# Hybrid decoder step on one core: the loads at the start on one queue in order of use, and the FFN's entry on VectorE

## The chip, the core and the metric

The kernel runs on 1 core of one Trainium2 chip. The metric is the time of one execution in device microseconds (us); the time of a kernel is the median of its runs. A profiled execution gives the trace, and the profile is read from it. The engines of the core are TensorE (PE: matmuls, and PEld: its weight loads), VectorE (DVE), ScalarE (ACT), GpSimd (POOL) and SyncE (SP), which here only issues DMAs.

## The reference

One layer of a decoder, for 256 prompt tokens and 8 x 8 sample tokens (320 in all), with D = 2048, a mixed width of 4096 and d_ff = 5632. All weights and inputs are float32.

```python
h    = rms_norm(x, norm_mix_pre)
proj = h @ w_in                                  # gMLP u | gMLP v | z | xBC | dt
gate_out, chunk_v = chunk_spatial_gate(gelu(u), gelu(v), ...)   # layer norm of v, 128-token mixing
ssm_out, states   = ssd_mixer(z, conv(xBC), dt, ...)            # Mamba-2 SSD, exact
mix = concat([gate_out, ssm_out]) @ w_out
x   = x + rms_norm(mix, norm_mix_post)
up, new_conv = causal_depthwise_conv(rms_norm(x, norm_ffn_pre) @ ffn_w_up, ...)
f   = (gelu_tanh(g) * u) @ ffn_w_down            # g, u = halves of up
x   = x + rms_norm(f, norm_ffn_post)
```

The outputs are x for prompt and sample tokens, the SSM states, the last rows of both convolutions and of v.

## The kernel before

**Tiling.** Activations stand transposed: 128 rows of a feature block by 320 tokens, so D is 16 blocks ("k-tiles", KD). A product needs float32 accuracy, so activations and weights are split into a high and a low part. A weight piece of up to 512 KB (a *slab*, `slab`, L108 to L119) is loaded by SyncE into `wraw` (L115, 3 buffers), cast by ScalarE to `whi` (L117, 3 buffers), and VectorE subtracts to get `wlo` (L119, 3 buffers). For each 128 x 128 block of it, `accumulate` runs three matmuls over 320 columns: whi by x hi (L128), whi by x lo (L129), wlo by x hi (L130). `project` runs one output group of 4 blocks (512 columns), slab by slab along k; a slab is 2 k-tiles by 4 blocks or 4 k-tiles by 2 blocks, that is 24 matmuls. PSUM has 4 banks for groups (`mm`) and 4 for the rest (`ms`).

**Order of the stages.** In-projection (gMLP v, then u and the SSD inputs), gMLP and SSD mixing, `w_out` in 8 chunks (`chunk_out`), the second root-mean-square root, the FFN's entry, 11 FFN groups of 512 + 512 columns, the last norm and the output. Each norm's factor is per token, so it commutes with the projection: the products run on the unscaled x, and the factor (`r1`, `r3`) is multiplied in when a PSUM bank is evacuated.

**What sets the order.** A scheduler places instructions by priority; `first()` and `tc.high_priority` raise it, and `tc.issue_after(i)` puts an instruction behind `i` on the same engine (it does nothing between two engines). Background tasks (`bg`, `tick`) are generators of which one step is emitted after each slab. Instructions of one engine, DMA issues among them, go out in order; a slab's DMA waits for its `wraw` buffer, which VectorE's `wlo` of three slabs before sets free.

**The start.** `ones` is filled and EARLY matmuls (L70, each two in the trace) keep TensorE busy until data is there. x (transposed, 2.63 MB) comes in six DMAs of 1, 1, 2, 4, 4, 4 k-tiles on ScalarE's queue (L523 to L529), the weight slabs on SyncE's. `x_ready` (L533) splits each k-tile of x: ScalarE `h_hi` (L537), VectorE `h_lo` (L538). The first `project` runs 4 slabs of one k-tile, 4 of two, and the last four k-tiles in two slabs, 192 matmuls. x by token (2.62 MB, six loads into `acc_mix`, `bT` and `cT`, needed for the first norm's squares) is loaded by GpSimd through the software queue (`load_by_token`, L548 to L552). A small copy of `h_hi` in k-tile 8 stands ahead of each load, so that they start after that split. `with_r1` squares them (L557), takes the root, spreads it over the partitions and evacuates the first group.

**Roots.** `rsqrt_of` works on VectorE alone. `rsqrt_by_root` (L237) uses ScalarE's square root, whose table has to be loaded first. `root_table(pd_last[-1])` asks for a tiny square root (`root_there`) behind a matmul of TensorE, so as to have the table there in time.

**The FFN's entry.** With `r2b`, the second root spread to all partitions, `x1_ready` (L975) makes x1 = acc * norm * r2b + x for each k-tile: VectorE scales (L980); the add of x (L981) is VectorE's for k-tiles 0 and 1 and GpSimd's for the other 14; then `split` makes ScalarE's `h_hi` (L346) and VectorE's `h_lo` (L347). `project(ffn_w_up, 0, ..., more=DFF)` runs six blocks (288 matmuls) while this goes on. ScalarE squares each k-tile of x1 (L281) for the third norm; the sums go to two totals, even k-tiles to `sq3` by GpSimd and odd ones to `sq3b` by VectorE (L282), behind the add of k-tile 11. `ffn_up(0)` goes on with the seventh block (`ps_one`) and the eighth (`ps_other`); in the seventh stand the token sums of both totals (L263, `tsum`), the third root, its spread to `r3`, and the evacuation (`evac`) of the first seven blocks.

In both stages GpSimd also has small work: pads of the convolution (L1017, L1018), and in the entry four updates of sample states (L1120).

Of the kernel before, what the change touches and what calls it, by code (L numbers as in the profile page):

```python
# [28 lines left out]
EARLY = 10  # L29
# [5 lines left out]
def hybrid_step(  # L35
# [201 lines left out]
    def rsqrt_by_root(rest, ps, scale, rows=P):  # L237

        v = tp.tile([P, 3], F32, tag="rs_v3", name="rs_v")[:rows]
        r = tp.tile([P, 3], F32, tag="rs_r3", name="rs_r", bufs=3)[:rows]  # L240
        t = tp.tile([P, 3], F32, tag="rs_t3", name="rs_t")[:rows]
        s = tp.tile([P, 3], F32, tag="rs_s3", name="rs_s")[:rows]
        dve.tensor_scalar(out=v, in0=rest, scalar1=scale, scalar2=EPS, op0=ALU.mult, op1=ALU.add)
        dve.scalar_tensor_tensor(out=v, in0=ps, scalar=scale, in1=v, op0=ALU.mult, op1=ALU.add)
        act.activation(s, v, AF.Sqrt)
# [30 lines left out]
    def add_square(total, x, begins, adder=pool, place=("sq", 2)):  # L276
        if begins:
            act.activation(total, x, AF.Square)
        else:
            sq = tp.tile([P, NT], F32, tag=place[0], name="sq", bufs=place[1])  # L280
            act.activation(sq, x, AF.Square)  # L281
            adder.tensor_tensor(out=total, in0=total, in1=sq, op=ALU.add)  # L282

    def squares_of(total):
# [3 lines left out]
        def step(nb):  # L288
            if nb < KD - 3:
                add_square(total, acc[:, nb, :], nb == 0)  # L290
                return
            with first():
                if nb < KD - 1:
                    held.append(misc("sq_ps")[:, :NT])
                else:
                    one.append(tp.tile([P, NT], F32, tag="sq", name="sq", bufs=2))
                act.activation((one or held)[-1], acc[:, nb, :], AF.Square)
                if nb > KD - 3:
                    dve.tensor_tensor(out=total, in0=total, in1=held.pop(0), op=ALU.add)
# [40 lines left out]
    def split(hi, lo, x, scale=None):  # L340
# [4 lines left out]
        else:  # L345
            act.activation(hi, x, AF.Copy, scale=scale)  # L346
            dve.scalar_tensor_tensor(out=lo, in0=x, scalar=scale, in1=hi.bitcast(F32), op0=ALU.mult, op1=ALU.subtract)  # L347

# [19 lines left out]
    with ExitStack() as mctx:  # L368
# [141 lines left out]
        with tc.tile_pool(name="gp", bufs=1) as gp:  # L510
# [11 lines left out]
            k = 0  # L522
            with tc.high_priority(offset=300000):  # L523
                for n in (1, 1, 2, 4, 4, 4):
                    cs = slice(KD + NT * k if k else 0, KD + NT * (k + n))
                    act.dma_start(flat[:, cs], xT[:, cs])
                    k += n
                    if k == 2:
                        act.activation(held, ones[:, 0:1], AF.Square)  # L529
# [3 lines left out]
            def x_ready(k0, nk):  # L533
                with tc.high_priority(offset=100000):
                    for kt in range(k0, k0 + nk):
# [11 lines left out]
            by_tok += [(t.rearrange("p k n -> p (k n)")[64:, :D // 2], slice(64, P), slice(NP, NT), 2, i) for i, t in enumerate((bT, cT))]  # L547
            def load_by_token():  # L548
# [27 lines left out]
            load_by_token()  # L576

            def with_r1():
                yield
# [114 lines left out]
        with tc.tile_pool(name="sd", bufs=1) as sd:  # L694
# [250 lines left out]
            root_table(pd_last[-1])  # L945
# [7 lines left out]
            with first():  # L953
# [6 lines left out]
                r = rsqrt_by_root(most, ps, 1.0 / D)  # L960
# [8 lines left out]
            xr, added = {}, []  # L969
# [5 lines left out]
            def x1_ready(k0, nk):  # L975
                for kt in range(k0, k0 + nk):
                    q, k = kt // 4, kt % 4
                    a = acc[:, kt, :]
                    with first() if kt < 2 else tc.high_priority(offset=100000):
                        dve.scalar_tensor_tensor(out=a, in0=a, scalar=col(prm_at["norm"][0] + kt), in1=r2b, op0=ALU.mult, op1=ALU.mult)  # L980
                        added.append((dve if kt < 2 else pool).tensor_tensor(out=a, in0=a, in1=xr[q][:, k, :], op=ALU.add).ins)  # L981
                        split(hT[0][:, kt, :], hT[1][:, kt, :], a, col(prm_at["norm"][1] + kt))
# [13 lines left out]
    with tc.tile_pool(name="fp", bufs=1) as fp:  # L996
# [5 lines left out]
        def ffn_up(g):  # L1002
# [41 lines left out]
            if g == 0:  # L1044

                ps = misc("ps_one")
                for i in range(2):
# [92 lines left out]
        for g in range(NG):  # L1140
# [5 lines left out]
            if g == NG - 1:  # L1146
                finish(grow)
                root_table(pd_last[-1])
# [19 lines left out]
        r = rsqrt_by_root(most, ps, 1.0 / D)  # L1168
# [108 lines left out]
```

## Time and profile before

| what | value |
|---|---|
| median of 3 runs | 1811.83 us (1809.76 to 1812.11) |
| profiled execution, its own time | 1812.42 us |
| its span (first to last instruction) | 1810.7 us |
| TensorE matmuls busy | 1784.3 us (99%) |
| VectorE, ScalarE, GpSimd busy | 1183.4, 798.7, 303.2 us |
| mean DMA rate | 169 GB/s |

How to read the profile: a group's row gives line, engine, operation, output and inputs, shapes and count, then the busy time and the mean ns of one, then the idle time of the engine before them and what ended it. A row of the chain of waits gives a start, a length and the work that the next step waited for; a row of the timeline gives start, length, engine, line and operation, and in brackets the idle time before it with its releaser. In the table by stretches each engine has its busy time and its number of instructions, then come TensorE's granted clock, the share of the DMA engines' time and the GB/s. Matmuls are pipelined, so a matmul is shown longer than its distance from the next.

### The profile page before, as it was taken

The numbers are of one execution on the slowest core, as the hardware profiler recorded it, in microseconds if no ns is written. First come the engines' busy times: TensorE is split into PE (matmuls) and PEld (weight loads), VectorE is DVE, ScalarE is ACT, GpSimd is POOL, SyncE is SP. The second block draws the span as 40 slices with busy tenths as digits, with TensorE's granted clock in tenths as the row PEclk, the third lists the DMA queues.
The fourth block names the chain that finished last, engine by engine and source line by source line (L and its number), as shares of the span: only waits on it lengthen the run. The fifth ranks groups of instructions, "written<-read, shape, count | busy, mean of one in ns | idle before, by whom it ended". The sixth has DMA issues, their size and how long they took to land.

```text
span 1810.7 us, 31220 instructions
## 1 busy us (share of the span) xinstructions
PE 1784.3 (99%) x12222; PEld 1750.2 (97%) x12222; DVE 1183.4 (65%) x2033; ACT 798.7 (44%) x1106; POOL 303.2 (17%) x624
## 2 busy tenths in 40 slices
PE   8999999999999999999999999999999999999998
PEld 7999999999999898998899999999999999999997
DVE  4449565556867778577776575757665565756575
ACT  6444454334535354445455444344434343433335
POOL 2102110000120111005622212121201020101004
PEclk9999999999999999999999999999999999999999
DMA  8545544445764644454556656565654444444442
GB/s 269 178 149 176 173 137 152 152 151 162 244 197 154 192 161 150 137 178 150 161 163 201 196 191 211 174 202 177 194 175 151 147 153 150 155 152 153 149 153 99
DMA packets 229779, 306.46 MB, mean 169 GB/s; under 512 B 17440, under 2 KB 152704, under 8 KB 229440
## 3 DMA queue, kind: packets, MB, share of 16 engines
q1 hardware_dynamic: 216384, 279.26, 48.5%
q10 hardware_dynamic: 11024, 18.10, 2.7%
q0 software_dynamic: 2224, 7.11, 1.4%
q8 instruction: 96, 1.57, 0.4%
q14 instruction: 51, 0.42, 0.1%
HBM read 286.85 MB, written 17.58 MB: 168 GB/s over the span
## 4 chain that ended last, share of the span: by engine, by line
PE 93%; DVE 2%; DMA 2%; ACT 1%; POOL 1%; issue 1%; ACTq 0%; DVEq 0%; POOLq 0%
PE ps L128 19%; PE ps L130 19%; PE ps L129 19%; PE pd L128 10%; PE pd L130 10%; PE pd L129 10%; DMA wraw<-in_w_in 1%; PE y_ps L851 1%; DVE wlo L119 1%; POOL acc_mix L981 1%; PE yo_ps L804 1%; ACT whi L117 0%; PE sg L658 0%; PE up_ps L1128 0%; PE xt_ps L357 0%
## 5 line engine op out<-in xcount | busy, mean ns | idle before, releaser
L119 DVE TENSOR_TENSOR wlo<-wraw,whi 128x1024 fp32r<-128x1024 f32 (+1 forms) x476 | 591.4, 1243 | 409.1 <-ACT whi L117 406.1
L117 ACT CAST whi<-wraw 128x1024 fp32r<-128x1024 f32 (+1 forms) x476 | 496.8, 1044 | 721.1 <-PE ps L129 443.4
L128 PE MATMUL ps<-h_hi,whi 128*128 128x320 f32 x2528 | 790.2, 313 | 11.0 <-ACT whi L117 7.6
L130 PE MATMUL ps<-h_hi,wlo 128*128 128x320 f32 x2528 | 786.5, 311 | 4.0 <-DVE wlo L119 4.0
L129 PE MATMUL ps<-h_lo,whi 128*128 128x320 f32 x2528 | 785.1, 311 | 0.0
L128 PEld LDWEIGHTS ps<-h_hi,whi 128*128 128x128 f32 x2528 | 477.8, 189 | 17.6 <-ACT whi L117 9.2
L130 PEld LDWEIGHTS ps<-h_hi,wlo 128*128 128x128 f32 x2528 | 477.8, 189 | 6.1 <-DVE wlo L119 5.9
L129 PEld LDWEIGHTS ps<-h_lo,whi 128*128 128x128 f32 x2528 | 477.8, 189 | 1.2 <-issue 0.5
L128 PE MATMUL pd<-fhi,whi 128*128 128x320 f32 x704 | 218.0, 310 | 0.0
L129 PE MATMUL pd<-flo,whi 128*128 128x320 f32 x704 | 217.9, 310 | 0.0
L130 PE MATMUL pd<-fhi,wlo 128*128 128x320 f32 x704 | 217.9, 309 | 0.0
L128 PE MATMUL pd<-ohi,whi 128*128 128x320 f32 x448 | 140.6, 314 | 0.0
L129 PE MATMUL pd<-olo,whi 128*128 128x320 f32 x448 | 139.0, 310 | 0.0
L130 PE MATMUL pd<-ohi,wlo 128*128 128x320 f32 x448 | 138.7, 310 | 0.0
L129 PEld LDWEIGHTS pd<-flo,whi 128*128 128x128 f32 x704 | 132.2, 188 | 0.7
L130 PEld LDWEIGHTS pd<-fhi,wlo 128*128 128x128 f32 x704 | 132.2, 188 | 0.0
L128 PEld LDWEIGHTS pd<-fhi,whi 128*128 128x128 f32 x704 | 132.2, 188 | 0.0
L211 DVE TENSOR_TENSOR acc_ffn<-acc_ffn,pd 128x320 f32<-128x320 f32 x160 | 77.1, 483 | 35.8 <-PE pd L130 34.8
L1032 POOL COPY ptf<-pad 128x2 f32<-128x2 f32 x88 | 23.0, 263 | 390.7 <-DVE pad L1020 390.0
L128 PEld LDWEIGHTS pd<-ohi,whi 128*128 128x128 f32 x448 | 84.1, 188 | 4.0 <-issue 2.5
L130 PEld LDWEIGHTS pd<-ohi,wlo 128*128 128x128 f32 x448 | 84.1, 188 | 0.6 <-issue 0.6
L129 PEld LDWEIGHTS pd<-olo,whi 128*128 128x128 f32 x448 | 84.2, 188 | 0.2 <-issue 0.2
(296 smaller groups left out, 1596.1 us busy)
## 6 DMA issues: line engine op xcount, KB each, us to landing
wraw<-in_ffn_w_up SPq DMA_DIRECT2D x176, 512.0 KB, 3.5
wraw<-in_w_in SPq DMA_DIRECT2D x144, 512.0 KB, 3.5
wraw<-in_ffn_w_down SPq DMA_DIRECT2D x88, 512.0 KB, 3.3
wraw<-in_w_out SPq DMA_DIRECT2D x64, 512.0 KB, 3.3
st<-in_state_ssm SPq DMA_DIRECT2D x64, 256.0 KB, 3.7
out_ssm_state_sample<-st ACTq DMA_DIRECT2D x32, 256.0 KB, 2.5
cs<-dacs_d SPq DMA_DIRECT2D x16, 320.0 KB, 3.5
xr<-in_xT SPq DMA_DIRECT2D x4, 640.0 KB, 4.6
```

The costliest lines, as they stand in the source:

```text
L117: act.copy(hi[:, :m], raw[:, :m])
L119: dve.tensor_tensor(out=lo[:, :m], in0=raw[:, :m], in1=hi[:, :m].bitcast(F32), op=ALU.subtract)
L128: pe.matmul(ps, whi, xhi, start=first, stop=False)
L129: pe.matmul(ps, whi, xlo, start=False, stop=False)
L130: return pe.matmul(ps, wlo, xhi, start=False, stop=last).ins
L211: dve.tensor_tensor(out=acc[:, nb, :], in0=acc[:, nb, :], in1=ps[:, :NT], op=ALU.add)
L804: pe.matmul(ps_yo[row:row + 32, :256], cms[:, 4 * h + i, :], st[h][:, 256 * r:256 * r + 256], start=i == 0, stop=i == 3, tile_position=(0, ...
L851: pe.matmul(ps[64 * i:64 * i + 64, cols], w(hl), x(hl, m, cpx), tile_position=(0, 64 * i), **flags)
L981: added.append((dve if kt < 2 else pool).tensor_tensor(out=a, in0=a, in1=xr[q][:, k, :], op=ALU.add).ins)
L1032: pool.tensor_copy(ptf[:, k, :], pad[:, 256:258])
```

## The change

1. At the start SyncE's queue takes all of the loads, in order of use: x of the first k-tile, its slab, x of the second, its slab, and so on. x is loaded inside `x_ready`, with the piece of k-tiles that the next slab needs. The loads by token follow: one each ahead of the slabs of k-tiles 8 and 10 in the source, two with the last four k-tiles, the rest behind. In the order in which SyncE issues them the first stands behind the slab of k-tiles 8 and 9, and the last two among the slabs of the next projection. GpSimd's six loads and copies go. EARLY is 8, and `with_r1` begins one step later.
2. `root_table` stands behind ScalarE's square of the fourth last block of the sum (in `squares_of`), no longer behind a matmul of TensorE.
3. In the entry VectorE does all 16 adds of x1 and all 15 square adds, into one total; ScalarE's squares stand behind its cast of k-tile 11 (the first five) or 15 (the others; `split` returns that cast), the square adds behind VectorE's add of k-tile 11. The third root moves in the source: token sums stand behind the seventh block, `spread` and the evacuations in the middle of the eighth; block 0 of the first six is copied from its bank to SBUF by ScalarE (`raw`) and evacuated from there.

```diff
-EARLY = 10
+EARLY = 8
...
-    def rsqrt_by_root(rest, ps, scale, rows=P):
+    def rsqrt_by_root(rest, scale, ps=None, rows=P):
...
-        dve.scalar_tensor_tensor(out=v, in0=ps, scalar=scale, in1=v, op0=ALU.mult, op1=ALU.add)
+        if ps is not None:
+            dve.scalar_tensor_tensor(out=v, in0=ps, scalar=scale, in1=v, op0=ALU.mult, op1=ALU.add)
...
             if nb < KD - 3:
-                add_square(total, acc[:, nb, :], nb == 0)
+                made = add_square(total, acc[:, nb, :], nb == 0)
+                if nb == KD - 4:
+                    root_table(made)
                 return
...
-            k = 0
             with tc.high_priority(offset=300000):
-                for n in (1, 1, 2, 4, 4, 4):
-                    cs = slice(KD + NT * k if k else 0, KD + NT * (k + n))
-                    act.dma_start(flat[:, cs], xT[:, cs])
-                    k += n
-                    if k == 2:
-                        act.activation(held, ones[:, 0:1], AF.Square)
+                act.activation(held, ones[:, 0:1], AF.Square)
...
             def x_ready(k0, nk):
                 with tc.high_priority(offset=100000):
+                    cs = slice(KD + NT * k0 if k0 else 0, KD + NT * (k0 + nk))
+                    sp.dma_start(flat[:, cs], xT[:, cs])
+                    for _ in range({8: 1, 10: 1, 12: 2}.get(k0, 0)):
+                        load_by_token()
...
             def load_by_token():
-                for t, _, rows, c, i in by_tok:
-
-                    pool.tensor_copy(t[:, 0:1], hT[0][:, 8, 0:1][t.shape[0] % P:].bitcast(F32))
-                    pool.dma_start(t, x_tok[rows, D // 2 * i:D // 2 * (i + 1)])
+                if to_load:
+                    t, _, rows, _, i = to_load.pop(0)
+                    sp.dma_start(t, x_tok[rows, D // 2 * i:D // 2 * (i + 1)])
...
-            load_by_token()
+            with tc.high_priority(offset=100000):
+                while to_load:
+                    load_by_token()
 
             def with_r1():
+                yield
                 yield
...
-            root_table(pd_last[-1])
             squares, one = squares_of(sq2)
...
-                        added.append((dve if kt < 2 else pool).tensor_tensor(out=a, in0=a, in1=xr[q][:, k, :], op=ALU.add).ins)
-                        split(hT[0][:, kt, :], hT[1][:, kt, :], a, col(prm_at["norm"][1] + kt))
+                        added.append(dve.tensor_tensor(out=a, in0=a, in1=xr[q][:, k, :], op=ALU.add).ins)
+                        whole.append(split(hT[0][:, kt, :], hT[1][:, kt, :], a, col(prm_at["norm"][1] + kt)))
...
-            sq3b = tp.tile([P, NT], F32, tag="pv", name="sq3b", bufs=4)
-            with tc.issue_after(added[11]):
-                for kt in range(KD):
-                    add_square((sq3, sq3b)[kt % 2], acc[:, kt, :], kt < 2, (pool, dve)[kt % 2], ("pv", 4))
+            for kt in range(KD):
+                with tc.issue_after(added[11]), tc.issue_after(whole[11 if kt < 5 else KD - 1]):
+                    add_square(sq3, acc[:, kt, :], kt < 1, dve, ("pv", 4))
...
-                    if i == 0:
-                        with first():
-                            r = rsqrt_by_root(token_sums(sq3), token_sums(sq3b), 1.0 / D)
+                up0.append((None, 6, ps))
+                raw = fp.tile([P, NT], F32, name="raw")
+                act.copy(raw, up0[0][2][:, :NT])
+                up0[0] = (None, 0, raw)
                 with first():
-                    spread(r, r3)
-                up0.append((None, 6, ps))
-                for _, j, ps in up0:
-                    evac(j // 4, j % 4, ps)
+                    r = rsqrt_by_root(token_sums(sq3), 1.0 / D)
...
+                    if i == 0:
+                        with first():
+                            spread(r, r3)
+                        for _, j, up in up0:
+                            evac(j // 4, j % 4, up)
                 evac(1, 3, ps)
...
             if g == NG - 1:
                 finish(grow)
-                root_table(pd_last[-1])
```

More of the change, by code (lines that the diff above doesn't have):

```diff
@@ L277, in add_square @@
         if begins:
[L278 to L282, printed above, removed]
+            return act.activation(total, x, AF.Square).ins
+        sq = tp.tile([P, NT], F32, tag=place[0], name="sq", bufs=place[1])
+        made = act.activation(sq, x, AF.Square).ins
+        adder.tensor_tensor(out=total, in0=total, in1=sq, op=ALU.add)
+        return made
     def squares_of(total):
@@ L345, in split @@
         else:
-            act.activation(hi, x, AF.Copy, scale=scale)
+            made = act.activation(hi, x, AF.Copy, scale=scale).ins
             dve.scalar_tensor_tensor(out=lo, in0=x, scalar=scale, in1=hi.bitcast(F32), op0=ALU.mult, op1=ALU.subtract)
+            return made
     def out_parts(pool_, name):
@@ L547, in hybrid_step @@
             by_tok += [(t.rearrange("p k n -> p (k n)")[64:, :D // 2], slice(64, P), slice(NP, NT), 2, i) for i, t in enumerate((bT, cT))]
+            to_load = list(by_tok)
             def load_by_token():
-                for t, _, rows, c, i in by_tok:
-                    pool.tensor_copy(t[:, 0:1], hT[0][:, 8, 0:1][t.shape[0] % P:].bitcast(F32))
-                    pool.dma_start(t, x_tok[rows, D // 2 * i:D // 2 * (i + 1)])
+                if to_load:
+                    t, _, rows, _, i = to_load.pop(0)
+                    sp.dma_start(t, x_tok[rows, D // 2 * i:D // 2 * (i + 1)])
             def x_squares():
@@ L959, in hybrid_step @@
                     made = next(rest[0])
-                r = rsqrt_by_root(most, ps, 1.0 / D)
+                r = rsqrt_by_root(most, 1.0 / D, ps)
                 behind = rsqrt_ins[-1]
@@ L966, in hybrid_step @@
             sq3 = hp.tile([P, NT], F32, tag="ssq", name="sq3")
-            xr, added = {}, []
+            xr, added, whole = {}, [], []
             def load_x(q):
@@ L1167, in hybrid_step @@
             ps = token_sums(*one)
-        r = rsqrt_by_root(most, ps, 1.0 / D)
+        r = rsqrt_by_root(most, 1.0 / D, ps)
         with tc.issue_after(sums_ins[-1]):
```

## The prediction

> **What bounds the kernel now.** The page first: its busy times, then its chain of waits by engine.
>
> ```profile
> PE 1784.3 (99%) x12222; PEld 1750.2 (97%) x12222; DVE 1183.4 (65%) x2033; ACT 798.7 (44%) x1106; POOL 303.2 (17%) x624
> PE 93%; DVE 2%; DMA 2%; ACT 1%; POOL 1%; issue 1%; ACTq 0%; DVEq 0%; POOLq 0%
> ```
>
> TensorE is the bound, and only the stretches where it stands still, or runs at half clock, can give time back. The table by stretches (busy us, instructions in brackets, granted clock, DMA share, GB/s) shows where they are:
>
> ```profile
> 5.70:44.70 39.00, 31.80 (x193) 29.84 (x194) 20.53 (x39) 25.99 (x43) 7.89 (x16) 0.96 0.88 274
> 843.20:848.60 5.40, 5.40 (x21) 5.40 (x22) 4.96 (x9) 3.83 (x10) 4.13 (x4) 0.51 0.19 36
> 870.50:883.60 13.10, 8.58 (x51) 7.25 (x51) 8.85 (x13) 7.27 (x14) 9.72 (x16) 0.96 0.55 171
> 883.60:889.50 5.90, 5.90 (x22) 5.90 (x23) 5.84 (x4) 1.70 (x3) 5.90 (x5) 0.50 0.71 209
> 1000.00:1700.00 700.00, 700.00 (x4760) 698.88 (x4759) 442.98 (x710) 277.94 (x342) 105.39 (x279) 1.00 0.53 171
> ```
>
> Between 1000 and 1700 us nothing is to be had: 4760 matmuls in 700 us, 0.147 us each. That is the price of one below. The first projection, 192 matmuls in the 39.0 us from 5.70 to 44.70, would need 192 x 0.147 = 28.2: 10.8 us are lost. At the FFN's entry there is idle time (4.5 of 13.1 us) and then half clock (22 matmuls in 5.9 us, 2.7 more than at full clock).
>
> The chain of waits of 0 to 46 us names the first loss; the DMA issues of the first 45 us, and of the whole page, price it:
>
> ```profile
> 7.47 7.27 DMA wraw<-in_w_in
> 17.17 13.20 DMA wraw<-in_w_in
> ```
> ```profile
> wraw<-in_w_in SPq DMA_DIRECT2D x10, 512.0 KB, 5.6
> acc_mix<-in_x_tok POOLq DMA_DIRECT2D x4, 512.0 KB, 6.9
> ```
> ```profile
> wraw<-in_w_in SPq DMA_DIRECT2D x144, 512.0 KB, 3.5
> ```
>
> A weight slab that lands in 3.5 us elsewhere takes 13.2 while x by token (2.6 MB) goes through the software queue beside it: the bytes needed last share the 16 engines with those needed first.
>
> The groups between 841 and 897 us, busy us, mean ns and idle time before them, show the entry:
>
> ```profile
> L119 DVE TENSOR_TENSOR wlo<-wraw,whi 128x1024 fp32r<-128x1024 f32 x12 | 18.2, 1527 | 3.1 <-ACT whi L117 3.0
> L981 POOL TENSOR_TENSOR acc_mix<-acc_mix,xr 128x320 f32<-128x320 f32 x14 | 16.3, 1181 | 10.0 <-DVE acc_mix L980 10.0
> L347 DVE SCALAR_TENSOR_TENSOR h_lo<-acc_mix,prm,h_hi 128x320 fp32r<-128x320 f32 x16 | 13.0, 828 | 1.6 <-ACT h_hi L346 1.6
> L346 ACT ACTIVATE h_hi<-acc_mix,prm 128x320 fp32r<-128x320 f32 x16 | 8.9, 562 | 17.5 <-POOL acc_mix L981 14.6 <-DVE acc_mix L981 2.9
> L282 POOL TENSOR_TENSOR sq<-sq,sq 128x320 f32<-128x320 f32 x7 | 8.6, 1232 | 3.3 <-ACT sq L281 3.3
> L980 DVE SCALAR_TENSOR_TENSOR acc_mix<-acc_mix,prm,spread 128x320 f32<-128x320 f32 x16 | 8.0, 539 | 0.0
> L1120 POOL TENSOR_TENSOR st<-st,kept 128x512 f32<-128x512 f32 x4 | 6.8, 1721 | 0.0
> L282 DVE TENSOR_TENSOR sq3b<-sq3b,sq 128x320 f32<-128x320 f32 x7 | 4.3, 610 | 3.2 <-ACT sq L281 3.1
> L981 DVE TENSOR_TENSOR acc_mix<-acc_mix,xr 128x320 f32<-128x320 f32 x2 | 0.9, 482 | 0.0
> ```
>
> ScalarE's cast of each block waits 14.6 us for GpSimd's add at 1181 ns, which VectorE does in 482; ScalarE's squares wait for GpSimd's too, and ScalarE is the one that casts the weights.
>
> **The start, part A.** The x loads leave ScalarE's queue and the loads by token leave the software queue; both go to SyncE's, in the order in which TensorE wants them. The program's first DMAs, two groups of the first 45 us, one stretch where SyncE's queue moved nearly all the bytes, two where the software queue ran beside it, and one behind those:
>
> ```profile
> 0.82 1.34 SPq L115 DMA_DIRECT2D wraw<-in_w_in  x3
> ```
> ```profile
> 0.81 3.37 DMA vt<-in_xT
> ```
> ```profile
> L538 DVE SCALAR_TENSOR_TENSOR h_lo<-vt,h_hi 128x320 fp32r<-128x320 f32 x16 | 8.2, 546 | 3.4 <-ACT h_hi L537 3.4
> L70 PE MATMUL early<-ones 128*128 128x128 f32 x20 | 4.5, 423 | 1.1 <-DVE ones L66 1.1
> ```
> ```profile
> 12.00:14.00 2.00, 0.56 (x2) 0.30 (x2) 0.62 (x2) 1.26 (x3) 0.00 (x0) 1.00 1.04 406
> 26.00:28.00 2.00, 1.75 (x12) 1.49 (x11) 0.00 (x0) 0.53 (x2) 0.00 (x0) 1.00 0.99 173
> 28.00:30.00 2.00, 0.00 (x0) 0.00 (x0) 0.00 (x0) 0.00 (x0) 0.00 (x0) 1.00 1.08 210
> 34.00:36.00 2.00, 2.00 (x9) 2.00 (x9) 1.49 (x2) 1.98 (x4) 0.00 (x0) 0.50 0.83 263
> ```
>
> An issue takes 0.45 us, so 18 issues before the last slab of the first projection take 8 us, well inside 26. Up to that slab 8.92 MB pass (x 2.63, weights 4.19, four token loads 2.10). The 3.5 us of a slab elsewhere, less 0.52 MB at 0.38 MB/us (a little under the 406 GB/s), leave 2.1 us, which I split into 1.1 before the first byte and 1.0 after the last. So first bytes at 1.9 us, and 1.05 for the cast: ready at 1.9 + 23.5 + 1.0 + 1.05 = 27.4. TensorE comes to it after 168 of the 192 matmuls. It starts when the warm-up matmuls end: 20 of them take 4.5 us before, from 1.1 on; 16 (EARLY 8, not 10) end 0.9 earlier, at about 4.75. The first x and weight (0.43 MB) land at 1.9 + 1.1 + 1.0 = 4.0 and are cast at 4.6. So it needs the last slab at 4.75 + 0.26 (the first lo part) + 168 x 0.147 = 29.7: 2.3 us of slack. The same sum for the slabs before it gives slacks of 0 to 3 us, least where k-tiles 4 and 5 come (cast at 11.3, wanted at 12.2). So TensorE goes through, and the projection ends at 4.75 + 0.26 + 28.2 = 33.2 instead of 44.7: -11.5, with the half clock of the 34 to 36 us row in it. The token squares go between ScalarE's casts and the first root comes a tick later: up to 0.6 of new stall, so **-10.9**. The bounds: with 0.31 MB/us (274 GB/s over 0.88 busy) the last slab is ready at 32.7, 24 matmuls take 3.5, and with the new stall it is -7.9; without one, -11.5.
>
> The Trainium skill, "DMA: Bandwidth & Descriptors", section "Issuing engines are not separate DMA queues", says that DMAs of all issuing engines run on the same 16 engines and interleave, so that several issuers only save issue time. The trace agrees in the 13.2 us landing; by that rule one queue gives up 8 us of hidden issue time and nothing else, and the gain is one of order. Its section "Bandwidth" gives 341 GB/s for 1 MB transfers; by that the last slab is cast at 30.1, and the gain 0.4 us less.
>
> **The square-root table, part B.** Two loads near 38 us go, where ScalarE waits anyway: 0. At 838.16 and at the end a load stands in the chain:
>
> ```profile
> 838.16 1.28 ACT L245
> 843.14 1.97 PE ps L128 x6
> ```
> ```profile
> 839.06 0.16 DVE L244 SCALAR_TENSOR_TENSOR rs_v<-tsum,rs_v 128x3 f32<-128x3 f32 x1 [1.01 <-PE tsum L263]
> ```
> ```profile
> 1794.68 1.28 ACT L245 ACT_TABLE_LOAD   x1
> ```
> ```profile
> 1794.99 0.16 DVE L244 SCALAR_TENSOR_TENSOR rs_v<-tsum,rs_v 128x3 f32<-128x3 f32 x1 [1.16 <-PE tsum L263]
> ```
>
> At the end the root's input is there at 1795.15 and the load ends at 1795.96: loading before the last three squares gives **-0.75** (-0.8 to 0). At 838 the sums are there at 839.2 and the load ends at 839.44, so 0.2 can be had, while the load now delays a weight cast and the last squares: **+0.1** (-0.2 to +0.9).
>
> **The entry, part C.** VectorE takes all 16 adds and all 15 square adds. Its first steps, and a weight's lo part over the whole page:
>
> ```profile
> 841.09 1.00 DVE L980 SCALAR_TENSOR_TENSOR acc_mix<-acc_mix,prm,spread 128x320 f32<-128x320 f32 x2
> 842.01 0.88 DVE L981 TENSOR_TENSOR acc_mix<-acc_mix,xr 128x320 f32<-128x320 f32 x2
> ```
> ```profile
> L119 DVE TENSOR_TENSOR wlo<-wraw,whi 128x1024 fp32r<-128x1024 f32 (+1 forms) x476 | 591.4, 1243 | 409.1 <-ACT whi L117 406.1
> ```
>
> Its work from T0 (841.09) to the last square: 16 x (0.50 scale + 0.44 add + 0.50 lo) + 11 wlo at 1.24 + 15 square adds at 0.48 = 43.9 us. The 0.50 and 0.44 are distances of neighbours (two in 1.00, two in 0.88); the lo part takes 546 ns at the start, where GpSimd is nearly idle, less the overlap of neighbours; 0.48 is the add's 482. GpSimd's four updates at 1721 ns stay and slow it, for some 2.5 us: 46.4. TensorE: first matmul at T0 + 2.05, as before, 288 x 0.147 = 42.3, and 2.4 for half clock from 843 on (21 matmuls in 5.4), which stays since the wait before it does: T0 + 46.8. Both end close together, so I add 0.9 and 1.0, for wlo that come late and for the token sums that wait for the last square: T0 + 48.7. Before:
>
> ```profile
> 896.87 0.56 PE tsum L263 x6
> 897.97 0.56 PE tsum L263 x6
> ```
>
> The first sums were at about T0 + 55.6: -6.9. The second set of sums goes (one total instead of two): -0.6. The third root in the eighth block waits for nobody but the evacuations, and block 0 is copied out so that its bank is free: 0 (0 to +0.7). **C: -7.5**, -9 at the best. The worst: GpSimd's neighbourhood was not what slowed VectorE, and 16 x (0.54 + 0.48 + 0.83) + 11 x 1.53 + 15 x 0.61 = 55.6 us of VectorE stand there, as much as before: 0.
>
> The Trainium skill, "SBUF — State Buffer", section "Who interferes with whom", has a VectorE instruction with two SBUF inputs and a GpSimd one that reads SBUF exclude each other for whole instructions. The 1527 against 1243 ns agrees; by it the four updates could cost up to 6.8 us instead of 2.5, and C would be -3.6.
>
> **Sum.** -10.9 + 0.1 - 7.5 - 0.75 = -19 from the profiled execution's own 1812.42 (span 1810.7, 1.7 around it, kept): 1793.4. The median of the runs shown is 1811.83, 0.6 below it. I say 1793.5. The clock's half-speed stretches (2.4 us lost at 843, 2.7 at 884) can fall otherwise: 1.5 either way.
>
> **The rivals.** (1) One queue delivers 0.31 MB/us: A is -7.9, giving **1796.5**. For it: 274 GB/s over that stretch. Against: 406 GB/s where SyncE's queue was nearly alone. (2) VectorE becomes the bound of the entry, by its own work or by exclusion through GpSimd's updates: C between -3.6 (all 6.8 us of the updates) and 0, giving **1797.5 to 1801**. For it: 46.4 against TensorE's 46.8 leaves 0.4. Against: it waits 3.1 + 3.2 us in the rows above for others. Both together: 1804. (3) **Slower**: token loads stand ahead of slabs on one queue, so its rate decides all. The projection ends as before when 8.92 MB take 44.7 - 3.5 (24 last matmuls) - 1.05 - 1.0 - 1.9 = 37.2 us: 0.24 MB/us. At the 173 GB/s of 26 to 28 us it would end at 59, +14.3, and with the other parts' -8.15 the time is **1818.5**. Against: both low stretches had the software queue in them, which goes. (4) The change does not do what it says: the scheduler holds token loads or the square adds back, leaving only the table's -0.7 and a few us: **1809 to 1812**.
>
> **How the numbers follow.** Forecast (1789 to 1795.5) 0.6; (1) 0.14; (2) 0.11; both 0.04; (3) 0.06; (4) 0.05. From 1787.5 up to 1804 lie the first four, 0.89 less what their tails lose: that is the range. A measurement of this kernel tells 0.2% (3.6 us) from no change. Faster by more: 0.9; within: 0.05; slower: 0.05.
>
> **What would show it.** A: slabs land in 3.5 to 6 us up to 30 us, no gap of TensorE over 1 us after 6, 192 matmuls done by 34, no half clock near 33. If slabs land later with the DMA share at 1.0 and under 320 GB/s, rival 1 or 3. B: the load stands before the last squares, and ScalarE's root follows its input within 0.1 us. C: first token sums at T0 + 47.5 to 50, lo parts near 550 ns, no stall of GpSimd's, no half clock at 884; rival 2 shows TensorE waiting for wlo or h_lo with VectorE over 95% busy. I am wrong if TensorE's matmuls in the entry themselves get dearer, or time comes out in stages that the diff does not touch.

## The result, and the profile after

The changed kernel takes 1795.70 us (median of 4 runs, 1795.07 to 1796.77), the kernel before 1811.66 beside it: a ratio of 0.9915, interval 0.9897 to 0.9932. The profiled execution took 1795.42 with a span of 1793.7, 17.0 less than before's. The forecast was 1793.5 in a range of 1787.5 to 1804.

The places in time come from the order of TensorE's instructions: "matmul n" is the one that has n matmuls of the real work ahead of it, without warm-up, token sums and spreads (the first projection is 0 to 191).

| us | matmul 0 | 144 | 168 | 216 | 1000 | 2000 | 5600 | 6500 | last |
|---|---|---|---|---|---|---|---|---|---|
| before | 5.70 | 37.63 | 41.15 | 48.19 | 162.33 | 311.08 | 818.63 | 969.95 | 1804.69 |
| changed | 4.77 | 28.69 | 33.73 | 41.70 | 155.84 | 302.99 | 810.77 | 953.59 | 1787.54 |
| difference | -0.9 | -8.9 | -7.4 | -6.5 | -6.5 | -8.1 | -7.9 | -16.4 | -17.15 |

So the start gives 6.5 us, and had given 8.9 before 2.4 of it were lost between matmuls 144 and 216. Then 1.6 come off at 250 us, in a stage that the diff does not touch, 8.5 at the FFN's entry and 0.8 at the end.

The page's busy times:

```profile
PE 1774.8 (99%) x12212; PEld 1742.6 (97%) x12212; DVE 1186.2 (66%) x2053; ACT 796.5 (44%) x1106; POOL 271.7 (15%) x591
```

TensorE is busy for 9.5 us less, mostly since at half clock a matmul counts as busy for longer; GpSimd has given 31.5 us away. The start first, in the table by stretches of the changed kernel (busy us with instructions for TensorE, its weight loads, VectorE, ScalarE, GpSimd; then granted clock, DMA share, GB/s):

```profile
4.77:38.00 33.23, 29.89 (x192) 28.26 (x193) 18.73 (x28) 22.55 (x36) 3.33 (x7) 1.00 0.97 307
2.00:14.00 12.00, 10.48 (x62) 9.50 (x61) 6.08 (x12) 6.67 (x14) 3.67 (x14) 1.00 0.90 283
14.00:28.00 14.00, 13.58 (x92) 13.50 (x93) 8.83 (x12) 10.31 (x18) 0.00 (x0) 1.00 1.02 377
12.00:14.00 2.00, 1.20 (x9) 0.93 (x7) 0.05 (x1) 0.68 (x1) 0.00 (x0) 1.00 0.95 299
26.00:28.00 2.00, 2.00 (x16) 2.00 (x15) 0.80 (x2) 2.00 (x5) 0.00 (x0) 1.00 1.03 380
28.00:30.00 2.00, 2.00 (x14) 1.77 (x13) 1.69 (x2) 2.00 (x6) 0.00 (x0) 1.00 1.11 208
30.00:32.00 2.00, 2.00 (x16) 2.00 (x15) 0.55 (x1) 1.09 (x3) 1.25 (x1) 1.00 1.12 272
32.00:34.00 2.00, 0.86 (x7) 0.60 (x6) 0.29 (x1) 1.34 (x2) 0.55 (x1) 1.00 1.04 177
```

The projection's 192 matmuls take 33.2 us, not 39.0, and the half clock is gone. But the queue moves 307 GB/s, not 380. Only from 14 to 28 us does it come to the forecast's rate (377); up to 14 us it moves 283, and between 28 and 34 us it falls to 177 to 272 with its share at 1.0 to 1.1: the DMA engines are busy, the bytes are not coming. The DMA issues of the first 40 us:

```profile
wraw<-in_w_in SPq DMA_DIRECT2D x10, 512.0 KB, 6.7
acc_mix<-in_x_tok SPq DMA_DIRECT2D x4, 512.0 KB, 8.9
bT<-in_x_tok SPq DMA_DIRECT2D x1, 256.0 KB, 12.4
```

The last slab of the first projection is issued at 20.5 us, and TensorE, which wants it at 32.3, waits for its cast (timeline of ScalarE):

```profile
32.63 1.04 ACT L117 CAST whi<-wraw 128x1024 fp32r<-128x1024 f32 x1 [1.54 <-PE ps L130]
```

The bracket names TensorE because a matmul was the last event of the profile before the cast. Of the slab loads issued from 15 to 45 us the longest took 12.0 us to land, which fits this one (20.5 + 12.0):

```profile
DMA to landing us min/median/max: 4.4/6.6/12.0
```

The matmuls that had to free its `whi` buffer had ended at about 25 us: the wait is for the DMA.

The entry, from 833 to 885 us, in groups:

```profile
L119 DVE TENSOR_TENSOR wlo<-wraw,whi 128x1024 fp32r<-128x1024 f32 x13 | 17.4, 1346 | 0.1
L282 DVE TENSOR_TENSOR sq<-sq,sq 128x320 f32<-128x320 f32 x15 | 8.7, 580 | 1.0
L349 ACT ACTIVATE h_hi<-acc_mix,prm 128x320 fp32r<-128x320 f32 x16 | 8.0, 553 | 4.6 <-DVE acc_mix L986 4.5
L350 DVE SCALAR_TENSOR_TENSOR h_lo<-acc_mix,prm,h_hi 128x320 fp32r<-128x320 f32 x16 | 8.0, 546 | 2.9 <-ACT h_hi L349 2.9
L986 DVE TENSOR_TENSOR acc_mix<-acc_mix,xr 128x320 f32<-128x320 f32 x16 | 7.0, 486 | 0.0
```

The lo parts take 546 ns (828 before), ScalarE's casts wait 4.6 us for the adds (17.5), and the half clock near 884 us is gone. By stretches, the entry and the half clock at its beginning, which stayed:

```profile
840.50:884.00 43.50, 43.13 (x296) 42.90 (x295) 39.44 (x64) 24.40 (x42) 9.74 (x14) 1.00 0.61 188
835.30:840.50 5.20, 5.16 (x19) 5.16 (x20) 5.20 (x13) 1.46 (x3) 0.00 (x0) 0.50 0.33 97
```

The first token sums start 47.4 us after the first scaling (833.29), and they still wait, 0.36 us on the profile, for the last square add (timeline of TensorE):

```profile
880.66 0.80 PE L264 MATMUL tsum<-ones,sq 128*128 128x1 f32 x6 [0.36 <-DVE sq L282]
```

At the end the root follows its input at once: VectorE's row, then ScalarE's, with no table load between.

```profile
1778.63 0.16 DVE L245 SCALAR_TENSOR_TENSOR rs_v<-tsum,rs_v 128x3 f32<-128x3 f32 x1 [1.16 <-PE tsum L264]
```
```profile
1778.82 0.20 ACT L246 ACTIVATE rs_s<-rs_v 128x3 f32<-128x3 f32 x1 [0.52 <-DVE rs_v L245]
```

The 1.6 us at 250 are a half-clock stretch that before had and the changed kernel has not. Before, then changed, at about the same work:

```profile
251.20:254.50 3.30, 3.30 (x14) 3.30 (x13) 0.30 (x2) 0.32 (x3) 0.47 (x2) 0.50 0.31 111
```
```profile
242.00:249.00 7.00, 7.00 (x53) 6.59 (x53) 2.62 (x9) 2.72 (x6) 0.46 (x2) 1.00 0.30 91
```

### The profile page after: what moved, and what is told of

Read it like the earlier page. It is cut to its first block, busy times and chain, and to the rows that moved or that the text cites. A ratio compares the mean times of both kernels' runs of the same rounds, so it can differ in the third digit from the quotient of the medians.

```text
span 1793.7 us, 31203 instructions
## 1 busy us (share of the span) xinstructions
PE 1774.8 (99%) x12212; PEld 1742.6 (97%) x12212; DVE 1186.2 (66%) x2053; ACT 796.5 (44%) x1106; POOL 271.7 (15%) x591
## 4 chain that ended last, share of the span: by engine, by line
PE 88%; issue 6%; DVE 3%; DMA 2%; ACT 1%; SPq 0%; POOL 0%; DVEq 0%; ACTq 0%; POOLq 0%
PE ps L128 18%; PE ps L130 18%; PE ps L129 18%; PE pd L128 10%; PE pd L130 10%; PE pd L129 10%; PE y_ps L857 1%; DVE wlo L119 1%; ACT whi L117 1%; DMA wraw<-in_w_in 1%; PE yo_ps L810 1%; PE sg L664 0%; PE up_ps L1135 0%; DVE sq L282 0%; PE xt_ps L361 0%
## 5 line engine op out<-in xcount | busy, mean ns | idle before, releaser
L119 DVE TENSOR_TENSOR wlo<-wraw,whi 128x1024 fp32r<-128x1024 f32 (+1 forms) x476 | 591.3, 1243 | 396.1 <-ACT whi L117 393.2
L128 PEld LDWEIGHTS ps<-h_hi,whi 128*128 128x128 f32 x2528 | 475.5, 188 | 12.1 <-issue 5.1
```

What stands on the lines that cost most here:

```text
L119: dve.tensor_tensor(out=lo[:, :m], in0=raw[:, :m], in1=hi[:, :m].bitcast(F32), op=ALU.subtract)
L128: pe.matmul(ps, whi, xhi, start=first, stop=False)
```

## The experiments

The theory after the result: the start falls short because token loads stand ahead of the last slab on one queue that moves less than was assumed; the entry gains because GpSimd is off its chain. Rivals: SyncE's waiting in order, the loads to 64 partitions, and a gain of the entry that really is the squares' or the clock's. The kernel before was timed beside each set of experiments: a median of 1808.84 beside the first four, one run of 1807.3 beside the next four, 1809.28 beside the last three.

**The parts alone: only_start and only_entry.** The kernel before with the pieces of the diff from `x_ready`, `load_by_token`, `with_r1` and EARLY; and with those of `x1_ready`, the squares and `ffn_up(0)`.

> The kernel before with the start's part of the change alone (loads on SyncE's queue in order of use, EARLY 8, with_r1 a step later). If the parts add up: matmul 216 about 6.5 us earlier than before, as in the whole change, and 6.5 to 8 us off the time (1804 to 1805.5), the 1.5 being the half-clock stretch near 251 us that the whole change lost too. If the start's gain needs the other parts, or is given back before the entry, under 3 us.

> The kernel before with the FFN entry's part alone (adds and squares on VectorE, third root moved); start and root tables as before. If the parts add up: first token sums 47 to 48 us after the first scaling (55.6 before), 8 to 9 us off the time (about 1803). If the entry's gain came from elsewhere (the clock, other phase of the weight loads after the faster start), 3 to 5 us.

only_start takes 1804.86 (ratio 0.9979, interval 0.9970 to 0.9988), only_entry 1802.77 (0.9967, 0.9954 to 0.9980), beside 1808.84: -4.0 and -6.1. These are less than the 6.5 to 8 and the 8 to 9 expected. In only_start matmul 216 comes at 41.70, just as in the whole change, and in only_entry the token sums come 48.0 us after the first scaling, against 54.8 in only_start. Together with the 0.8 at the end the parts make -10.9; the whole change makes -12.1 beside the 1809.28 (below). So they add up, within 1.2 us; the 0.8 is from the first pair of profiles, as no run has the square-root table's part alone. One reason for the smaller sizes is that the kernel before is 2 to 3 us faster here: with its start unchanged, only_entry's matmul 216 comes at 46.10, 2.1 us before the first profile's 48.19. In only_entry's profile 2.8 us of the entry's gain are lost again behind a 1.7 us wait for the last square add, where a stretch of half clock follows.

**Four token loads later: late_tok.**

```diff
-                    for _ in range({8: 1, 10: 1, 12: 2}.get(k0, 0)):
+                    for _ in range({8: 1, 10: 1}.get(k0, 0)):
...
             def with_r1():
                 yield
+                with tc.high_priority(offset=100000):
+                    while to_load:
+                        load_by_token()
                 yield
...
```

> The change with four of the six loads by token issued behind the first two slabs of the second projection, so that 1.05 MB less stand ahead of the last slab of the first projection. Theory (the one queue's bytes set when that slab lands): no gap of TensorE at 32 us, the first projection ends 2 to 2.5 us earlier, matmul 216 at about 39.5 instead of 41.7; time 1793 to 1794, if the later root costs nothing. Rival (the last slab was late for its own small pieces or for ScalarE's work, not for bytes ahead of it): the gap stays, matmul 216 within 0.5 us of the change's. Rival (the root comes late instead): the gain shows at matmul 216 and is gone at matmul 300.

Matmul 168 comes at 31.10 and 216 at 38.15, 3.5 us before the change's and 10.0 before the first profile of before; no gap at 32. At matmul 1000 it is all still there (152.19 against 155.84), so the later root costs nothing. The row of the stretch, where 218 matmuls fill 32.5 of 33.3 us:

```profile
4.90:38.15 33.25, 32.50 (x218) 31.82 (x217) 20.60 (x32) 24.10 (x39) 3.43 (x7) 1.00 0.97 322
```

So what stands on the queue around the last slab is the cause. That is two things at once: two loads of 512 KB ahead of the slab, and the two of 256 KB to 64 partitions, which the change issues right behind it (at 21.2 and 25.1 us) and late_tok at 29.0 and 29.6; wide_tok below parts them. The time is 1796.59 all the same (ratio 0.9929, 0.9913 to 0.9946), not 1793 to 1794, and so not to be told from the change's own: the profiled run (1797.44, the slowest of its four) loses some 5 us against the change in two places that no edit touches, both at half clock (3.2 between matmuls 1000 and 2000, 2.2 between 2000 and 5000).

```profile
240.30:247.10 6.80, 6.80 (x27) 6.74 (x27) 0.41 (x3) 1.39 (x4) 0.46 (x2) 0.50 0.33 103
649.90:653.30 3.40, 3.40 (x15) 3.40 (x15) 1.92 (x7) 1.04 (x1) 0.00 (x0) 0.50 0.80 226
```

They are two lengths and one of 3.4 us. TensorE's short waits before them (0.7 us at 237, 1.6 at 648) stand in the other runs as well, most often without a half clock behind: the first (an idle time of 0.4 us) is in all 13 profiles, and a half clock follows in 5 of them. The other three runs of late_tok were not profiled; why they took 1795.90 to 1796.68 stays open.

**Token loads back on the software queue: tok_pool.** `load_by_token` as before the change, the rest as changed.

> The change with the six loads by token left on GpSimd's software queue, behind the split of k-tile 8, as before; x and the slabs stay on SyncE's queue. If the gain at the start comes from the order of the token loads: a stall of 3 to 4 us near 27 us again and matmul 216 at 45 to 47 us (48.2 before, 41.7 changed). If it comes from x and slabs alternating in order of use, matmul 216 stays within 1 us of 41.7.

Matmul 216 at 47.14, a stall of 4.7 us at 25.4: nearly the whole gain of the start comes with the token loads' move. Whether by their place in the order or by leaving the software queue, this run does not tell; late_tok, which moves them on one queue, shows that the place counts. One run took 1804.13. In its chain of waits one of the token loads is the longest DMA:

```profile
23.39 12.74 DMA bT<-in_x_tok
```

**The sample tokens over all partitions: wide_tok.** The rate falls at the same place of the program in before and in the change, with and without the software queue: where the two loads of sample tokens (64 partitions) pass.

```diff
-            by_tok += [(t...[64:, :D // 2], slice(64, P), slice(NP, NT), 2, i) ...]
+            by_tok += [(t...[:, :D // 4], slice(64, P), slice(NT - P, NT), 2, i) ...]
...
```

The kernel leaves out half of the sample tokens' columns in the first norm's squares, so that ScalarE's two squares of them take 0.63 us in place of 1.06.

> The change with the two loads of sample tokens spread over all 128 partitions with 512 columns each (same bytes) in place of 64 partitions with 1024; it leaves out half of the columns of the sample tokens in the first norm's squares. If loads to 64 partitions are what makes the rate fall to 177 to 272 GB/s between 28 and 34 us: over 330 GB/s there, these loads land in 6 to 9 us (12.4), the last slab of the first projection lands 1 to 2 us earlier, matmul 216 at 40 to 41 (41.7). If it is the slab's own 1 KB pieces: rate and landing as in the change, matmul 216 within 0.4.

```profile
28.00:30.00 2.00, 1.90 (x13) 1.64 (x13) 1.73 (x3) 2.00 (x5) 0.00 (x0) 1.00 1.08 363
30.00:32.00 2.00, 2.00 (x15) 2.00 (x14) 0.57 (x2) 1.98 (x4) 1.54 (x1) 1.00 1.05 353
```

363 and 353 GB/s in place of 208 and 272, with as many bytes. It is one run, but six have the change's start with the loads to 64 partitions (the change twice, only_start, adds_pool, sq_pool, hold_pool), and their rates are 169 to 208 and 240 to 272. The last slab is cast at 30.7 instead of 32.6 (31.7 to 33.8 in the six), matmul 216 comes at 39.61 instead of 41.70 (40.7 to 44.3); these loads land in 10.4 and 8.4 us, a little longer than expected. Between matmuls 144 and 216 TensorE loses 0.8 us over its 72 x 0.147, against 2.4 in the change and nothing in late_tok: with the same bytes ahead of the slab, the loads to 64 partitions were the larger part of that stall. In late_tok the fall comes at 34 to 36 us (213 GB/s with the share at 1.04), where these two loads end. The Trainium skill, "SBUF — State Buffer", section "Door 1: The DMA port swizzle", says that partitions 64 to 127 reach only half of the 16 ports through which DMAs write, and gives 196 GB/s measured for partitions 0 to 63; the trace's 177 to 272 with the share at 1.0 agree as far as they go, for slabs share the queue there, and no run has such a load alone. The slab that shares the queue with them is held up too. The time (1797.81, one run, inside the 1795.07 to 1798.41 of the change's nine) does not follow: 1.7 us are lost at 50 us, where the evacuation comes late behind ScalarE, which sits in a wait for a small parameter load (waits of 36 to 60 us).

```profile
ACT a_bc L458 <- DMA a_bc<-in_ssm_a_log: 4.9, 1, 4.9
...
PE ps L128 <- DVE ev L340: 1.7, 1, 1.7
```

**Which half of the entry: adds_pool and sq_pool.** The change with one of GpSimd's two jobs given back.

```diff
-                        added.append(dve.tensor_tensor(out=a, in0=a, in1=xr[q][:, k, :], op=ALU.add).ins)
+                        added.append((dve if kt < 2 else pool).tensor_tensor(out=a, in0=a, in1=xr[q][:, k, :], op=ALU.add).ins)
```
```diff
-                    add_square(sq3, acc[:, kt, :], kt < 1, dve, ("pv", 4))
+                    add_square((sq3, sq3b)[kt % 2], acc[:, kt, :], kt < 2, (pool, dve)[kt % 2], ("pv", 4))
```

> The change with the 14 adds of x1 back on GpSimd; all square adds stay on VectorE, the third root as changed. If the adds on GpSimd were what cost time (ScalarE's casts wait for them, VectorE's parts slow down beside them): first token sums 53 to 56 us after the first scaling (47.4 in the change), h_lo near 800 ns (546), TensorE idle for 2 to 4 us and a half-clock stretch before them. If the squares were: sums at 48 to 50.

> The change with the squares in two totals again, even k-tiles on GpSimd, odd on VectorE; all adds of x1 stay on VectorE. If the adds were what cost time: first token sums 46.5 to 48.5 us after the first scaling, as in the change or a little earlier, since VectorE has 8 adds less. If the squares on GpSimd were (ScalarE's squares wait for them and hold the weight casts): 51 to 55.

First token sums after the first scaling: 54.8 with both jobs on GpSimd (only_start), 50.2 with the adds there, 46.9 with the squares there, 47.4 with neither. So the squares on GpSimd cost nothing once the adds are gone, and the adds alone cost 2.8 (1.8 against the slowest of the six runs with neither) and not all 8: neither expectation of adds_pool holds. The other 5 us come only with both jobs there and the entry's old order. The waits of only_start (834 to 890 us) show TensorE's loss there: it waits for weight casts and lo parts, while ScalarE, which casts, waits with its squares for GpSimd:

```profile
ACT sq L281 <- POOL sq L282: 3.5, 2, 2.6
...
PE ps L130 <- DVE wlo L119: 3.2, 3, 1.5
...
PE ps L128 <- ACT whi L117: 2.9, 2, 2.0
```

In sq_pool ScalarE's squares wait for GpSimd even longer (7.1 us), and TensorE waits 0.3 for weights: that wait alone costs nothing. Rows of adds_pool:

```profile
L986 POOL TENSOR_TENSOR acc_mix<-acc_mix,xr 128x320 f32<-128x320 f32 x14 | 16.1, 1171 | 10.9 <-DVE acc_mix L985 10.9
L349 ACT ACTIVATE h_hi<-acc_mix,prm 128x320 fp32r<-128x320 f32 x16 | 8.8, 561 | 14.7 <-POOL acc_mix L986 11.8 <-DVE acc_mix L986 2.9
L350 DVE SCALAR_TENSOR_TENSOR h_lo<-acc_mix,prm,h_hi 128x320 fp32r<-128x320 f32 x16 | 12.4, 799 | 1.0 <-ACT h_hi L349 1.0
```

With the adds back the lo parts take 799 ns again, and ScalarE waits 14.7 us; TensorE waits 2.7 us for wlo but falls to no half clock. Times of one run each: 1798.76 and 1795.79; the second is as the change's median. One thing is mixed in: in both, unlike before, the squares stand behind the cast of k-tile 15 or 11, and the third root stands later. So how those 5 us divide between the two jobs in one queue and the order of the squares is not shown.

**GpSimd held back until the squares are done: hold_pool.**

```diff
+            summed = tp.tile([P, 1], F32, name="summed", bufs=1)
+            gate = pool.tensor_copy(summed, sq3[:, 0:1]).ins
...
+                with tc.issue_after(gate):
                     pool.memset(pad[:, 0:2], 0.0)
                     pool.tensor_copy(tokp[:, :, 0:2], fst[:, half, j])
...
+                      with tc.issue_after(gate):
                         pool.tensor_tensor(out=by_head(st[h]), ...)
```

> The change with GpSimd's pad copies and state updates held back until the last square is added (a one-column copy of the finished sum stands ahead of them on GpSimd). Theory (what is left of the wait before the third root's token sums comes from VectorE's square adds running beside GpSimd, at 0.6 to 1.05 us each in place of 0.48): TensorE waits under 0.3 us there (0.67 in the change, 1.6 to 2.0 in three other runs with the same entry), square adds near 490 ns, no half clock behind. Rival (the squares wait for ScalarE's weight casts instead): the wait stays at 0.6 to 2. It may turn the wait into a later one, for the pads of the evacuation, up to 1 us.

The reason to try it, from late_tok: five square adds beside GpSimd's state updates take 5.24 us (VectorE's row, then GpSimd's), and TensorE waits 1.3 for them.

```profile
877.55 5.24 DVE L282 TENSOR_TENSOR sq<-sq,sq 128x320 f32<-128x320 f32 x5
```
```profile
876.73 3.10 POOL L1127 TENSOR_TENSOR st<-st,kept 128x512 f32<-128x512 f32 x2 [5.09 <-DMA st<-in_state_ssm]
```

In hold_pool the adds take 491 ns, the sums come 46.7 us after the first scaling, and TensorE waits for nothing there. But the updates now stand beside the root's tiny steps, 128 x 3 elements, and the spread comes 6.3 us behind the sums instead of 3.8:

```profile
883.51 0.16 DVE L247 RECIPROCAL rs_r<-rs_s 128x3 f32<-128x3 f32 x1
883.71 0.81 DVE L248 SCALAR_TENSOR_TENSOR rs_t<-rs_v,rs_r 128x3 f32<-128x3 f32 x1
884.56 0.98 DVE L249 TENSOR_TENSOR rs_t<-rs_t,rs_r 128x3 f32<-128x3 f32 x1
885.58 0.98 DVE L250 SCALAR_TENSOR_TENSOR rs_r<-rs_t,rs_r 128x3 f32<-128x3 f32 x1
```
```profile
881.46 5.08 POOL L1131 TENSOR_TENSOR st<-st,kept 128x512 f32<-128x512 f32 x4
```

The reciprocal, which reads one tensor, takes 0.16; the steps that read two take 0.8 to 1.0 where they took 0.16 in the changed kernel, up to nearly the time of one update (5.08 / 4 = 1.27). In the trace the last three updates end at 884.51, 885.52 and 886.54, and the three steps that read two at 884.53, 885.54 and 886.56: each VectorE step ends with the GpSimd instruction beside it. That is the rule of the Trainium skill that the prediction weighed ("SBUF — State Buffer", section "Who interferes with whom"), and these rows show it more sharply than 1527 against 1243 ns did. The wait became a later and larger one (2.7 us before the spread): at matmul 6000 this kernel is 0.3 us behind the change's profile, at 6500 2.2. One run took 1798.03, inside the change's own range.

**Both stalls removed: late_hold2 and late_ahead_hold2, beside the change itself.** late_tok, with the pads behind the last square add as in hold_pool, and the state updates behind GpSimd's copies of the eighth evacuation; the second also has `ahead=1` in the first `project`.

```diff
-                pool.tensor_copy(ptf[:, k, :], pad[:, 256:258])
+                filled.append(pool.tensor_copy(ptf[:, k, :], pad[:, 256:258]).ins)
...
+                      with tc.issue_after(filled[7]):
                         pool.tensor_tensor(out=by_head(st[h]), ...)
```

> The changed kernel once more, as the base for the next two on the same chip. As before: 1795 to 1797. Half-clock stretches outside the entry and the end may differ from the first profile's (none): each costs 1.5 to 2.5 us, and where they fall in a run is not set by the kernel alone if the theory holds that their grid runs free of it.

> The change with four loads by token behind two slabs of the second projection, GpSimd's pad copies behind the last square add, and its state updates behind the evacuations of FFN group 0. If both stalls that are left are as the runs before showed them (3.5 us at the start; 0.7 to 2 us of square adds beside GpSimd, and in hold_pool 3 us of small root steps at 0.98 us beside state updates): matmul 216 at 38 to 38.5 us (41.7), first token sums 46.5 to 47 us after the first scaling with no wait, their spread 3.3 us behind or less, 3 to 5 us off the changed kernel's time (1791 to 1793.5). If the gain is given back by half-clock stretches at the waits that remain, or the updates now press on the evacuations: within 1.5 us of the changed kernel.

> late_hold2 with x loaded one slab further ahead, so that x of k-tiles 4 and 5 is issued before the slab of k-tile 3, whose issue waits for a buffer. If SyncE's waiting in order is what makes TensorE stall at 12 to 13 us (0.9 to 1.5 us): no gap over 0.5 us there, 0.5 to 1 us better than late_hold2. If the bytes are: the gap stays and the first slab comes later, 0 to 0.5 us worse.

| beside before, 1809.28 | median | range | ratio to before, interval |
|---|---|---|---|
| the change again | 1797.18 (5) | 1796.80 to 1798.41 | 0.9932, 0.9919 to 0.9946 |
| late_hold2 | 1793.09 (4) | 1792.30 to 1794.38 | 0.9911, 0.9897 to 0.9924 |
| late_ahead_hold2 | 1793.33 (4) | 1792.88 to 1794.79 | 0.9913, 0.9899 to 0.9926 |

late_hold2 is 4.1 us faster than the change, no run of the one reaching one of the other. Most of it is the start's: against the change's two profiles its first scaling comes 2.8 and 5.0 us earlier and its last matmul 2.8 and 5.8, so that what follows gave 0 to 0.8. Matmul 216 comes at 39.38, not at 38 to 38.5: two of the early stalls (0.6 us at 6.7, 1.5 at 13.0) are there as in the change, which late_tok did not have in that size. In its entry the square adds take 490 ns and TensorE has no idle time from the first matmul to the sums:

```profile
L282 DVE TENSOR_TENSOR sq<-sq,sq 128x320 f32<-128x320 f32 x15 | 7.4, 490 | 1.0
```
```profile
832.50:877.30 44.80, 44.74 (x288) 44.74 (x289) 40.19 (x71) 24.63 (x44) 1.21 (x3) 0.94 0.62 186
```

Loading x further ahead changes nothing that can be told (1793.33): its stalls are 0.9 at 12.7 and 1.5 at 24.3, so SyncE's waiting in order is not shown to be the cause of the early stalls, and bytes remain the likelier one. The change's own second profile has matmul 216 at 44.25 (41.70 in the first) with a half clock at 37 us. So the start varies by 2 us and more from run to run: 46.1 and 48.2 with the start of before, 40.7 to 44.3 in the six profiles with the change's, 38.2 to 40.0 in the three with four token loads later.

## Why the prediction held, and where it did not

- **What bounds.** Right: TensorE's idle time and half clock at the start, the entry and the end were what there was to get, and nothing came out elsewhere but the clock's own 1.6 us at 250.
- **A, -10.9: wrong in size, -6.5.** The failed step is "0.38 MB/us", from which the last slab was to be cast at 27.4. It was cast at 32.6 to 33.7. The rate was 307 GB/s over the stretch, the value of the first rival, with -7.9 for A and 1796.5 for the whole, and the measured -6.5 is even below it; by the prediction's own sign (slabs late with the share at 1.0 and under 320 GB/s) this rival, given 0.14, is what happened at the start. The 0.38 was there from 14 to 28 us (377 GB/s) and neither before (283) nor behind (177 to 272). late_tok shows that what stands around the slab on the queue decides (-10.0 with four token loads later, close to the forecast), and wide_tok shows one thing that takes the rate down: half the partitions. The prediction read 173 and 210 GB/s at 26 to 30 us of before and put them down to the software queue ("which goes"); they came where the two loads to 64 partitions pass, which are still there, on another queue. The -6.5 itself is one pair of profiles out of starts that vary by 2 us and more; only_start's time gives -4.0.
- **The rule of one queue.** That order gives the gain agrees: tok_pool loses nearly all of it with x and slabs still in order, and late_tok adds to it by order alone. Whether a second issuing engine would save anything was not tried.
- **B: right.** 0 at 836 (the last matmul of the sum to the entry's first took 6.62 us before, 6.67 after), -0.8 at the end for -0.75.
- **C, -7.5: right, -8.5 in the first profile.** The sums come at 47.4 where 48.7 was forecast (47.4 to 48.4 in six runs with this entry). TensorE's 46.8 is confirmed: 46.7 to 47.1 in the three runs where the sums wait for nothing. VectorE's work was near its sum: it is busy for 43.4 us up to the sums in the change and for 42.2 in late_hold2, where GpSimd is held back, so GpSimd's neighbourhood took 1.2 there for the 2.5 allowed (2.1 in the change's second profile); the square adds take 580 ns for 490. Rival 2 was near: the wait for the last square add is 0.4 to 1.7 us, and in only_entry it tipped into a half clock.
- **The clock, 1.5 either way: near, but too narrow.** It gave 1.6 in the first profile and took some 5 in late_tok's.
- **The sum** came within 2 us (1793.4 against the profiled 1795.4), but by two errors of opposite sign: 4.4 too much at the start, less 1.0 too little at the entry and 1.6 of luck with the clock. The median of 1795.70 lies just above the 1789 to 1795.5 that the forecast had 0.6 for. Timed again, the change gains 12.1 us (1797.18 beside 1809.28) where the first set shows 16.0: some 4 us of the first gain are what these runs of before and of the change happened to take.

Open: what makes a short wait tip into a half clock in one run and not in the next was seen and not tried; nor was it settled what keeps the rate at 225 to 320 GB/s in the first 14 us.

## What to carry to other kernels

When transfers compete for one need, order them by use on one queue, and then count the bytes ahead of each slab at the rate that the queue really shows; what is not wanted until later goes behind. A load that fills only 64 partitions should be priced well below the queue's best rate (here 169 to 272 GB/s where such loads passed, 353 to 363 without), and it delays what shares its queue. A VectorE step that reads two tensors beside GpSimd's work can take as long as GpSimd's instruction, however small the step is (here 0.16 us became 0.98): place GpSimd's work where VectorE's chain is not the one waited for.

## What the runs showed of the hardware

- VectorE steps of 128 x 3 elements with two tensor operands took 0.81 to 0.98 us in place of 0.16 beside GpSimd's updates, each ending 0.02 us behind one of them; the reciprocal with one tensor operand kept 0.16.
- From 28 to 32 us, where two loads of 256 KB to 64 partitions passed, the queue moved 169 to 272 GB/s in six runs, and 353 to 363 with as many bytes to 128 partitions. The two landed in 10.9 to 13.8 us, against 8.4 to 10.4; with less queued ahead of them (late_tok) in 6.2 and 6.8.
- Before 1780 us half clock came in stretches of 3.4 and 6.8 us, and behind the same wait of 0.4 us at about 240 us in 5 of 13 profiles and not in the others.
